# The gated convolution of a decoder trunk: c and v gates with the activations held stationary, their product turned through DRAM, the b gate last

## The chip, the core and the metric

The kernel runs on one core of a Trainium2 chip. A core has five engines, each with its own queue of instructions that it works through in order: PE multiplies matrices (the profile shows its loads of the stationary operand as a line of their own, PEld), DVE (VectorE) and ACT (ScalarE) work elementwise, POOL (GpSimd) too, and SP (SyncE) here issues transfers only. They meet through semaphores. On-chip memory is SBUF, with 128 partitions; PE writes its sums to PSUM, from where DVE and ACT fetch them. The metric is the time of one execution in microseconds (us), as the device measures it.

## What is computed

A trunk of two layers over 256 tokens of width 1024: one layer with a short gated convolution, one with sparse attention, each between two half-step SwiGLU feed-forward networks (FFNs). The change lies in the convolution and in one detail of the attention's bias tables.

```python
def short_conv_mixer(x, w_in, conv_w, w_out):
    b_gate, c_gate, v = jnp.split(x @ w_in, 3, axis=-1)
    u = c_gate * v
    y = lax.conv_general_dilated(u, conv_w[:, None, :], window_strides=(1,),
                                 padding=[(CONV_WIDTH - 1, 0)],
                                 dimension_numbers=('NWC', 'WIO', 'NWC'),
                                 feature_group_count=D_MODEL)
    return (b_gate * y) @ w_out
...
        hn = rmsnorm(h, mix_norm[i])
        if i < N_A_LAYERS:
            h = h + short_conv_mixer(hn, conv_w_in[i], conv_w[i], conv_w_out[i])
```

The convolution has three taps per channel and looks back in time: y[t] = w0 u[t-2] + w1 u[t-1] + w2 u[t].

## The kernel before

**Number format.** Every float32 operand of a product is split in a high part (rounded to the format PE takes, by a cast on ACT) and a low part (the rest, by a subtraction on DVE). A product of x and w is summed from high x high, low x high and high x low. The residual stream h lies channels on partitions, tokens along the row (8 tiles of 128 channels x 256 tokens); `xs[k]` holds tile k of the normed stream as [high 256 tokens | low 256 tokens]. The norm's factor, the inverse root mean square R of each token, is not multiplied in ahead of the products but behind them.

**Weights.** `Stream` (L116) brings all weights in the order of their use. A transfer on SP fetches a chunk of 128 x 2048 numbers into one of three `ws` buffers; each chunk is two units of 1024 columns. `high` (L146) casts a unit into a `wh` buffer on ACT, `low` (L171) makes its `wl` on DVE. At most six units (NBUF) are in being: `done` gives units back, and `pump` then makes as many new ones. Their instructions stand in ACT's and DVE's queues at the place where the code called `pump`.

**Two forms of a projection.** In the first (`a_pass`, L346) the weights are stationary: for each of eight k, a block of 128 x 128 high weights is loaded and the whole of `xs[k]` (512 columns) streams past (L351), and then for each k a block of low weights with the 256 high columns (L356). The result has channels on partitions, and its two halves must be added up. In the second form, used in the FFNs (`ffn_tokens`, L432 to L434) and in a part of their output projection (L493 to L495), the activations are stationary: for each k and each half of the tokens, three products with 512 weight columns. The result has tokens on partitions and is complete; it must be turned. `turned` (L386) and `placed` (L397) do that: DVE transposes blocks of 32 x 32, a transfer writes the tile to DRAM, and a second one reads it back in runs of 32 numbers, with channels on partitions.

**The convolution** (L713 to L751) uses the first form throughout. A loop over the eight tiles f of 128 channels takes three units each, in the order c, v, b: `a_group` (L375) gives PE 24 products of 512 and 24 of 256 columns; c and v go to a pair of PSUM banks, b to a single one. For f = 0, the norm's row R and its square R2 are made between two products (`conv_mid`, L739). Behind the products `conv_evac` (L713) is woven with the weights' preparation: after each `yield` one unit is made. It adds the halves of c and v (`total`, L362, ACT and DVE), multiplies them and R2 on POOL (L718, L719), adds b's halves (L721, L722) and multiplies with R on POOL (L723), applies the three taps (L727 on ACT, L728 and L729 on DVE), multiplies y and b (L731), and splits the result into z[f] (`split`, L358: cast L359 on ACT, subtraction L360 on DVE).

**What follows** is the output projection (`out_proj`, L471, without `rest`). Its first pass takes four units and runs the first seven of z for three tiles and the first two for the fourth (L351, L356), then the rest of each (L351, L356) and its evacuation (L455); the other four tiles run one by one (L533, L539). Between, the next FFN's weights are prepared.

**Tables.** `tables` (L259) is a generator in three steps that loads small constants and prepares the attention's bias rows. The convolution's loop takes the first two steps at f = 1 and f = 6; the second FFN takes the last one. `load_bias` (L760) then reads bias tiles from DRAM during that FFN, one transfer for each of two halves for tiles 0 to 5, one for both halves for 6 and 7.

`_layout` (L1390) puts the weights on the host in the order in which they are taken.

Of the kernel before, what the change touches and what calls it, by code (L numbers as in the profile page):

```python
# [9 lines left out]
F32 = mybir.dt.float32  # L10
F32R = mybir.dt.float32r
I32 = mybir.dt.int32
AF = mybir.ActivationFunctionType
# [55 lines left out]
def trunk(ctx, tc, A, out):  # L69
# [12 lines left out]
    def mk(shape, tag, bufs, dt=F32, pool=None):  # L82
        uid[0] += 1
        return (pool or sb).tile(list(shape), dt, tag=tag, name=f"{tag}_{uid[0]}", bufs=bufs)
# [12 lines left out]
    def bank(shape=(P, 512)):  # L97
        return mk(shape, "a", 4, pool=ps)

    def bank2():  # L100
        return mk([P, 2, 512], "mm", 2, pool=ps)

    def act(shape=(P, 512), dt=F32R):
        return mk(shape, "act", 22, dt)
# [4 lines left out]
    def t1(shape=(P, T)):  # L109
        return mk(shape, "t1", 6)  # L110
# [148 lines left out]
    def tables():  # L259

        sy.dma_start(small, A["small"])
        rb, oh = t2([P, P]), t2()
        po.memset(rb, 0.0)
        po.memset(rb[NB:NB + 1, :16], NEG)
        sy.dma_start(rb[:NB, :16], A["rel_bias"])
        po.memset(oh, 0.0)
        sy.dma_start(oh[:NB + 1], A["onehot"])
        yield
        ohr, rbr = act(), act([P, 2, P])
        po.tensor_copy(out=ohr, in_=oh)  # L270
        ac.copy(rbr[:, 0], rb)
        ve.tensor_tensor(out=rbr[:, 1], in0=rb, in1=rbr[:, 0].bitcast(F32), op=ALU.subtract)
        yield
        pr = bank()
        for x in range(2):
            pe.matmul(pr, rbr[:, x], ohr, start=(x == 0), stop=(x == 1))
        row = t2()
        ac.activation(row[:16], pr[:16], AF.Copy, scale=-1.0)
        sy.dma_start(row_d, row[:16])
# [78 lines left out]
    def split(src, dst):  # L358
        ac.copy(dst[:, :T], src)  # L359
        ve.tensor_tensor(out=dst[:, T:], in0=src, in1=dst[:, :T].bitcast(F32), op=ALU.subtract)  # L360

    def total(o, n):  # L362

        r = t2([P, n, T])
        ac.copy(r, o[:, :, T:])
        ve.tensor_tensor(out=r, in0=o[:, :, :T], in1=r, op=ALU.add)
        return r

    def weave(gen, rest=True):
        for _ in gen:  # L370
            W.pump(1)
        if rest:
            W.pump()
# [336 lines left out]
    out_proj(hid, 0.5, nm, rest=rest)  # L710
    nm.halves()

    def conv_evac(f, ocv, ob, R, R2, zs):  # L713
        r = total(ocv, 2)
        yield
        u = mk([P, 768], "pr", 6)[:, :T + 2]
        po.memset(u[:, :2], 0.0)
        po.tensor_tensor(out=u[:, 2:], in0=r[:, 0], in1=r[:, 1], op=ALU.mult)  # L718
        po.tensor_tensor(out=u[:, 2:], in0=u[:, 2:], in1=R2, op=ALU.mult)  # L719
        b = t1()  # L720
        ac.copy(b, ob[:, T:])  # L721
        ve.tensor_tensor(out=b, in0=ob[:, :T], in1=b, op=ALU.add)  # L722
        po.tensor_tensor(out=b, in0=b, in1=R, op=ALU.mult)  # L723
        yield
        tap = [gt[:, G_CONV + 8 * a + f:G_CONV + 8 * a + f + 1] for a in range(3)]
        y = t1()
        ac.activation(y, u[:, 2:], AF.Copy, scale=tap[2])  # L727
        ve.scalar_tensor_tensor(out=y, in0=u[:, 1:T + 1], scalar=tap[1], in1=y, op0=ALU.mult, op1=ALU.add)  # L728
        ve.scalar_tensor_tensor(out=y, in0=u[:, 0:T], scalar=tap[0], in1=y, op0=ALU.mult, op1=ALU.add)  # L729
        yield  # L730
        ve.tensor_tensor(out=y, in0=y, in1=b, op=ALU.mult)  # L731
        z = act()
        split(y, z)
        zs.append(z)

    zs = []
    box = [None]

    def conv_mid():  # L739
        R = nm.rows()  # L740
        R2 = mk([P, T], "R", 2)
        po.tensor_tensor(out=R2, in0=R, in1=R, op=ALU.mult)
        box[0] = R, R2

    tab = tables()
    for f in range(8):
        if f in (1, 6):
            next(tab)
        ob, ocv = bank(), bank2()
        a_group([ocv[:, 0], ocv[:, 1], ob], xs, conv_mid if f == 0 else None)  # L750
        weave(conv_evac(f, ocv, ob, *box[0], zs))  # L751

    xs = new_xs()
    nm = Norm([(xs, G_FFN2)])
# [5 lines left out]
    def load_bias(j):  # L760
        pp, hg = divmod(j, 4)
        b = kt8[:, j, T:].rearrange("p (a n) -> p a n", a=2)
        src = bass.AP(tensor=row_d.tensor, offset=row_d.offset + (8 * pp + hg) * OHW,
                      ap=[[1, P], [4 * OHW, 2], [1, 256]])
        for a in range(2):
            if a == 0 or j < 6:
                sy.dma_start(b[:, a:] if j > 5 else b[:, a], src[:, a:] if j > 5 else src[:, a])
        bias[j] = b

    def c_bias(j):  # L770
# [613 lines left out]
def _rows(w):  # L1384

    k, m = w.shape[0] // 128, w.shape[1] // 128
    return w.reshape(k, 128, m, 128).transpose(1, 2, 0, 3).reshape(128, -1)


def _layout(i):  # L1390
    a = {n: np.asarray(v) for n, v in i.items()}
    x = a["x"][0].T.reshape(8, 128, 256).transpose(1, 0, 2)
    r = {}
    for n in ("ffn1", "ffn2"):
        w = a[n + "_w_in"]
        ins, outs = [], []
        for w, v, turn in zip(w.reshape(2, 1024, -1), a[n + "_w_out"], (0, n == "ffn2")):
            ins.append(w.reshape(8, 128, 2, NF // 2, 256).transpose(1, 3, 0, 2, 4).reshape(128, -1))
            v = v.reshape(-1, 4, 2, 32, 1024).transpose(0, 2, 3, 1, 4).reshape(-1, 1024)
            if turn:  # L1400
                outs.append(v.reshape(NF, 128, 2, 512).transpose(1, 2, 0, 3).reshape(128, -1))
                continue
            first = v[:, :512].reshape(FF, 2, 2, 32, 4).transpose(0, 1, 4, 2, 3).reshape(NF, 128, 512).transpose(1, 0, 2)
            v = v[:, 512:].reshape(NF, 128, 4, 128).transpose(1, 2, 0, 3)
            outs.append(np.concatenate([x.reshape(128, -1) for x in (first, v)], 1))
        r[n + "_w_in"], r[n + "_w_out"] = np.stack(ins), np.stack(outs)

    w = r["ffn1_w_in"][0][:, :8192].reshape(128, 2, 8, 512)
    rows, second = np.concatenate([x, w[:, 0]], 2).reshape(128, -1), w[:, 1].reshape(128, -1)
    w = a["conv_w_in"][0].reshape(8, 128, 3, 8, 128)  # L1410
    r["conv_w_in"] = np.concatenate([w[:, :, 1:], w[:, :, :1]], 2).transpose(1, 3, 2, 0, 4).reshape(128, -1)
    r["conv_w_out"] = _rows(a["conv_w_out"][0])
    w = a["w_kv"].reshape(8, 128, 3, 2, 256)
    parts = [p.reshape(8, 128, 512).transpose(1, 0, 2).reshape(128, -1) for p in (w[:, :, 1:, 0], w[:, :, 1:, 1])]
    r["w_kv"] = np.concatenate(parts + [_rows(w[:, :, 0].reshape(1024, 512))], 1)
    for n in ("cmp_w1_k", "cmp_w1_v"):
        r[n] = a[n].reshape(2, 16, 64, 128).transpose(0, 2, 1, 3).reshape(128, -1)
    w = a["attn_w_q"][0]
    q = w[:, :1024].reshape(8, 128, 2, 512).transpose(2, 1, 0, 3).reshape(2, 128, -1)
    gates = w[:, 1024:].reshape(1024, 16, 3)  # L1420
    gates = np.concatenate([gates[:, :, 1:2], gates[:, :, 0:1], gates[:, :, 2:3]], 2).reshape(1024, 48)
    r["attn_w_q"] = np.concatenate(q, 1)
    r["attn_w_g"] = gates.reshape(8, 128, 48).transpose(1, 0, 2).reshape(128, -1)
    r["attn_w_o"] = a["attn_w_o"][0].reshape(2, 2, 4, 64, 8, 128).transpose(1, 3, 4, 0, 2, 5).reshape(128, -1)
    r["rel_bias"] = a["rel_bias"]
    cols = [a[n].reshape(-1, 128).T for n in ("ffn1_norm", "mix_norm", "ffn2_norm", "kv_norm", "conv_w")]
    cols += [np.concatenate([a[n].reshape(-1, 64)] * 2, 1).T for n in ("attn_q_norm", "k_norm")]
    cols += [np.zeros((128, G_N - sum(c.shape[1] for c in cols)), np.float32)]
    rows = np.concatenate(cols + [rows], 1)
    r["first"] = np.concatenate([(second[:, 512 * lo:512 * hi] if which else rows[:, lo:hi]).reshape(-1) for which, lo, hi, _ in PIECES])  # L1430
    cols = [np.eye(128, dtype=np.float32)]
    cols += [a[n].reshape(2, 16, 64).transpose(0, 2, 1).reshape(128, 16) for n in ("cmp_pe_k", "cmp_pe_v")]
    cols += [a["cmp_w2_k"], a["cmp_w2_v"]]
    cols += [np.repeat((np.arange(128) >= 31).astype(np.float32)[:, None], S_N - S_CM, 1)]
    r["small"] = np.concatenate(cols, 1)


    lim = [16, 23, 32, 46, 64, 91, 128, 182]
    oh = np.zeros((NB + 1, OHW), np.float32)
    for c in range(OHW):  # L1440
        d = c - 127
        oh[NB if d < 0 else d if d < 16 else 15 + sum(d >= x for x in lim), c] = 1.0
    r["onehot"] = oh
    return r
# [19 lines left out]
```

## Time and profile before

| what | us |
|---|---|
| median of 3 runs (950.53 to 950.8) | 950.73 |
| the profiled execution, its own time | 950.93 |
| its span, first to last instruction | 949.1 |
| PE busy in the span | 944.6 |
| DVE busy in the span | 657.5 |
| ACT busy in the span | 532.4 |
| POOL busy in the span | 138.8 |

The profile gives busy time by engine, by stretches of time and by groups of like instructions, and the chain of waits that ended last. In a group's row, the line is that of the program, then engine, operation, what it writes <- what it reads, shapes and count; behind the bar the busy time in us, the mean duration of one in ns, and the idle time of the engine ahead of them with what ended it. Matmuls are pipelined: the duration of one is its latency, and the pitch from start to start, which the chain shows (start, us, what, count), is what it costs a busy PE.

### The profile page before, as it was taken

The numbers are of one execution on the slowest core, as the hardware profiler recorded it, in microseconds if no ns is written. First come the engines' busy times: TensorE is split into PE (matmuls) and PEld (weight loads), VectorE is DVE, ScalarE is ACT, GpSimd is POOL, SyncE is SP. The second block draws the span as 40 slices with busy tenths as digits, with TensorE's granted clock in tenths as the row PEclk, the third lists the DMA queues.
The fourth block names the chain that finished last, engine by engine and source line by source line (L and its number), as shares of the span: only waits on it lengthen the run. The fifth ranks groups of instructions, "written<-read, shape, count | busy, mean of one in ns | idle before, by whom it ended". The sixth has DMA issues, their size and how long they took to land.

```text
span 949.1 us, 12899 instructions
## 1 busy us (share of the span) xinstructions
PE 944.6 (100%) x4674; PEld 792.3 (83%) x4674; DVE 657.5 (69%) x1058; ACT 532.4 (56%) x895; POOL 138.8 (15%) x215
## 2 busy tenths in 40 slices
PE   9999999999999999999999999999999999999998
PEld 7888888888888888888888888888877888888887
DVE  7766665778896677647756676865679786776662
ACT  7554544555565455545647774644589764544450
POOL 2000000244520010001221022200238120000000
PEclk9999999999999999999999999999999999999999
DMA  7778876645546998777646977876511247998770
GB/s 312 237 228 279 253 258 219 228 171 200 181 165 233 267 292 253 225 269 222 222 159 207 276 229 248 271 251 191 212 50 32 103 177 233 275 284 260 232 268 23
DMA packets 154380, 206.35 MB, mean 217 GB/s; under 512 B 115740, under 2 KB 131228, under 8 KB 133837
## 3 DMA queue, kind: packets, MB, share of 16 engines
q1 hardware_dynamic: 154172, 205.27, 66.3%
q8 instruction: 37, 0.61, 0.2%
q10 hardware_dynamic: 144, 0.26, 0.1%
q14 instruction: 27, 0.21, 0.1%
HBM read 189.75 MB, written 15.24 MB: 216 GB/s over the span
## 4 chain that ended last, share of the span: by engine, by line
PE 99%; DMA 1%; ACT 0%; SPq 0%; issue 0%; DVE 0%
PE mm L432 16%; PE mm L434 16%; PE mm L433 16%; PE a L533 7%; PE mm L351 4%; PE a L351 4%; PE a L539 4%; PE mm L493 3%; PE mm L494 3%; PE mm L495 3%; PE a L592 2%; PE a L590 2%; PE a L591 2%; PE mm L656 2%; PE a L356 2%; PE mm L356 2%
## 5 line engine op out<-in xcount | busy, mean ns | idle before, releaser
L183 DVE TENSOR_TENSOR wl<-ws,wh 128x1024 fp32r<-128x1024 f32 x316 | 390.5, 1255 | 209.4 <-ACT wh L166 192.2
L166 ACT CAST wh<-ws 128x1024 fp32r<-128x1024 f32 x316 | 324.6, 1048 | 219.7 <-DMA ws<-in_ffn_w_in_dram 99.0
L432 PE MATMUL mm<-wh,xs 128*128 128x512 f32 x656 | 256.2, 391 | 0.0
L434 PE MATMUL mm<-wl,xs 128*128 128x512 f32 x656 | 255.7, 390 | 0.0
L433 PE MATMUL mm<-wh,xs 128*128 128x512 f32 x656 | 255.6, 390 | 0.0
L434 PEld LDWEIGHTS mm<-wl,xs 128*128 128x128 f32 x656 | 123.2, 188 | 26.2 <-DVE wl L183 0.4
L433 PEld LDWEIGHTS mm<-wh,xs 128*128 128x128 f32 x656 | 123.3, 188 | 25.2
L432 PEld LDWEIGHTS mm<-wh,xs 128*128 128x128 f32 x656 | 123.3, 188 | 25.1
L311 POOL TENSOR_TENSOR sq<-sq,t 128x256 f32<-128x256 f32 x42 | 34.8, 829 | 384.6 <-ACT t L309 383.9
L390 ACT ACTIVATE t<-mm,rc 128x256 f32<-128x256 f32 x86 | 40.6, 472 | 56.2 <-DVE t L391 47.6
L533 PE MATMUL a<-act,wh 128*128 128x512 f32 x296 | 69.5, 390 | 0.0
L533 PEld LDWEIGHTS a<-act,wh 128*128 128x128 f32 x296 | 55.0, 188 | 10.9
L391 DVE SCALAR_TENSOR_TENSOR t<-mm,rc,t 128x256 f32<-128x256 f32 x86 | 41.4, 482 | 15.5 <-ACT t L390 12.0
L493 PE MATMUL mm<-wh,act 128*128 128x512 f32 x132 | 51.4, 390 | 0.0
L494 PE MATMUL mm<-wh,act 128*128 128x512 f32 x132 | 51.4, 389 | 0.0
L495 PE MATMUL mm<-wl,act 128*128 128x512 f32 x132 | 51.4, 389 | 0.0
L359 ACT CAST act<-t 128x256 fp32r<-128x256 f32 x96 | 34.6, 405 | 26.3 <-DVE t L731 19.4
L294 ACT ACTIVATE xs<-base 128x256 fp32r<-128x256 f32 x48 | 24.1, 505 | 43.0 <-DVE base L455 27.3
L392 DVE STREAM_TRANSPOSE t<-t 128x256 f32<-128x256 f32 x88 | 39.2, 445 | 3.1
L360 DVE TENSOR_TENSOR act<-t,act 128x256 fp32r<-128x256 f32 x96 | 37.1, 424 | 4.4 <-ACT act L359 4.4
L539 PEld LDWEIGHTS a<-act,wl 128*128 128x128 f32 x296 | 37.2, 192 | 1.0
L539 PE MATMUL a<-act,wl 128*128 128x256 f32 x296 | 37.5, 283 | 0.0
(279 smaller groups left out, 1203.6 us busy)
## 6 DMA issues: line engine op xcount, KB each, us to landing
ws<-in_ffn_w_in_dram SPq DMA_DIRECT2D x84, 1024.0 KB, 5.7
ws<-in_ffn_w_out_dram SPq DMA_DIRECT2D x44, 1024.0 KB, 6.2
ws<-in_conv_w_in_dram SPq DMA_DIRECT2D x12, 1024.0 KB, 4.6
turn<-t SPq DMA_DIRECT2D x44, 256.0 KB, 2.2
t<-turn SPq DMA_DIRECT2D x44, 256.0 KB, 7.2
ws<-in_w_kv_dram SPq DMA_DIRECT2D x6, 1024.0 KB, 5.8
ws<-in_conv_w_out_dram SPq DMA_DIRECT2D x4, 1024.0 KB, 5.0
ws<-in_attn_w_q_dram SPq DMA_DIRECT2D x4, 1024.0 KB, 4.9
```

What stands on the lines that cost most here:

```text
L166: ac.copy(h, src)
L183: ve.tensor_tensor(out=l, in0=src, in1=h.bitcast(F32), op=ALU.subtract)
L351: pe.matmul(o, u[0][:, k * P:(k + 1) * P], xs[k], start=(k == 0), stop=False)
L391: ve.scalar_tensor_tensor(out=s, in0=o[tt][:, T:], scalar=rc[:, tt:tt + 1], in1=s, op0=ALU.mult, op1=ALU.mult)
L432: pe.matmul(o[tt], sh, wh, start=(k == 0), stop=False)
L433: pe.matmul(o[tt], sl, wh, start=False, stop=False)
L434: pe.matmul(o[tt], sh, wl, start=False, stop=(k == 7))
L493: pe.matmul(o[:, tt], sh, wh, start=(k == 0), stop=False)
L494: pe.matmul(o[:, tt], sl, wh, start=False, stop=False)
L495: pe.matmul(o[:, tt], sh, wl, start=False, stop=(k == NF - 1))
L533: pe.matmul(o, run[k][0], lhs[k], start=(k == 0), stop=(k == last))
L539: pe.matmul(o[:, :T], run[k][1], lhs[k][:, :T], start=False, stop=(k == last))
```

## The change

- c and v take the second form: four groups n = 0 to 3 of 512 channels (c, v of the first half of the channels, then c, v of the second half), 48 products of 512 columns each (`conv_tokens`). c is copied from PSUM by ACT (`gate`); v is multiplied by it and by the square of R as a column (`r2`, made by way of a small write to and read from DRAM) on DVE, transposed there, and written to DRAM, 256 KB for each half of the tokens (`conv_turned`).
- The reading back (`conv_placed`, two transfers) is issued in group n = 2 at k = 3 for the first half, and at f = 1 of the b gate for the second.
- The taps (`conv_taps`) of tiles 0 to 2 run in group n = 3, of 3 behind it, of 4 and 5 at f = 5 and of 6 and 7 at f = 6. The padding's columns fall away: the two DVE products shorten to 254 and 255 columns. y, not b, is multiplied by R on POOL.
- The b gate follows alone, eight times one unit by `a_pass`. `conv_sum` adds its halves, `conv_product` multiplies with y, `conv_split` splits one tile later than before (f - 1 at f). Weights are pumped after the evacuation, for f = 0 to 4 and 7 only.
- The evacuations of the c and v groups stand ahead of the weights' preparation in the queues.
- `load_bias`: tiles 4 and 5 are also read by one transfer.
- The host lays `conv_w_in` out anew.

```diff
-    def conv_evac(f, ocv, ob, R, R2, zs):
...
+    zs, Y, conv = [], [], {}
+    tab = tables()
+
+    def conv_tokens(o, step):
+
+        for k in range(8):
+            if k % 2 == 0:
+                u, = W.take()
+            wh, wl = [u[x][:, (k % 2) * 512:(k % 2 + 1) * 512] for x in range(2)]
+            for tt in range(2):
+                sh, sl = xs[k][:, tt * P:(tt + 1) * P], xs[k][:, T + tt * P:T + (tt + 1) * P]
+                pe.matmul(o[:, tt], sh, wh, start=(k == 0), stop=False)
+                pe.matmul(o[:, tt], sl, wh, start=False, stop=False)
+                pe.matmul(o[:, tt], sh, wl, start=False, stop=(k == 7))
+            if k % 2 == 1:
+                W.done(1, k < 7)
+            step(k)
+
+    def conv_turned(gate, o):
+        d = mk([2, 2, P, T], "conv", 2, pool=dr)
+        for tt in range(2):
+            tb = t2()
+            ve.scalar_tensor_tensor(out=gate[tt], in0=o[:, tt], scalar=conv["r2"][:, tt:tt + 1], in1=gate[tt],
+                                    op0=ALU.mult, op1=ALU.mult)
+            ve.transpose(tb, gate[tt])
+            sy.dma_start(d[:, tt].rearrange("m p n -> p m n"), tb.rearrange("p (m n) -> p m n", m=2))
+        return d
+
+    def conv_placed(d):
+        r = []
+        for m in range(2):
+            r.append(t2([P, 2, T]))
+            sy.dma_start(r[m].rearrange("p c (b j) -> p c b j", j=32),
+                         d[m].rearrange("t (b i) (x c j) -> (i x) c (t b) j", i=32, c=2, j=32))
+        return r
+
+    def conv_taps(f):
+
+        m, c = divmod(f, 2)
+        if c == 0:
+            Y.append(act([P, 2, T], F32))
         tap = [gt[:, G_CONV + 8 * a + f:G_CONV + 8 * a + f + 1] for a in range(3)]
...
+        u, y = conv["u", m // 2][m % 2][:, c], Y[m][:, c]
+        ac.activation(y, u, AF.Copy, scale=tap[2])
+        for a in range(2):
+            ve.scalar_tensor_tensor(out=y[:, 2 - a:], in0=u[:, :T - 2 + a], scalar=tap[a], in1=y[:, 2 - a:],
+                                    op0=ALU.mult, op1=ALU.add)
+        po.tensor_tensor(out=y, in0=y, in1=conv["R"], op=ALU.mult)
...
+    def conv_step(n, k):
+        if n == 0 and k == 5:
+            conv["R"] = R = nm.rows()
+            rd, rc, conv["r2"] = mk([1, T], "rd", 1, pool=dr), mk([P, 2], "rc", 2, pool=tiny), sm([P, 2])
+            sy.dma_start(rd, R[:1])
+            sy.dma_start(rc, rd.rearrange("o (t p) -> (o p) t", t=2))
+            po.tensor_tensor(out=conv["r2"], in0=rc, in1=rc, op=ALU.mult)
+        if n == 1 and k == 1:
+            next(tab)
+        if n == 2 and k == 3:
+            conv["u", 0] = conv_placed(conv.pop(("d", 0)))
+        if n == 2 and k == 5:
+            next(tab)
+        if n == 3 and k in (2, 4, 6):
+            conv_taps(k // 2 - 1)
+
+    for n in range(4):
+        o = bank2()
+        conv_tokens(o, lambda k: conv_step(n, k))
+        if n % 2 == 0:
+            gate = [t2() for _ in range(2)]
+            for tt in range(2):
+                ac.copy(gate[tt], o[:, tt])
+        else:
+            conv["d", n // 2] = conv_turned(gate, o)
+            del gate
+        W.pump()
+    conv_taps(3)
+    bs = {}
+
+    def conv_sum(f, o):
+        bs[f] = b = t1()
+        ac.copy(b, o[:, T:])
+        ve.tensor_tensor(out=b, in0=o[:, :T], in1=b, op=ALU.add)
+
+    def conv_product(f):
+        ve.tensor_tensor(out=bs[f], in0=bs[f], in1=Y[f // 2][:, f % 2], op=ALU.mult)
+
+    def conv_split(f):
+        zs.append(act())
+        split(bs.pop(f), zs[f])
+
     for f in range(8):
...
+        o, (u,) = bank(), W.take()
+        a_pass([(o, u, xs, range(8))])
+        W.done(1, False)
+        if f == 1:
+            conv["u", 1] = conv_placed(conv.pop(("d", 1)))
+        if f < 5:
+            if f:
+                conv_split(f - 1)
+            conv_sum(f, o)
+            if f < 4:
+                conv_product(f)
+            W.pump()
+        elif f == 5:
+            conv_taps(4)
+            conv_taps(5)
+            conv_sum(5, o)
+            conv_product(4)
+        elif f == 6:
+            conv_split(4)
+            conv_taps(6)
+            conv_taps(7)
+            conv_product(5)
+            conv_sum(6, o)
+        else:
+            conv_split(5)
+            conv_product(6)
+            conv_split(6)
+            conv_sum(7, o)
+            conv_product(7)
+            conv_split(7)
+            W.pump()
...
-            if a == 0 or j < 6:
-                sy.dma_start(b[:, a:] if j > 5 else b[:, a], src[:, a:] if j > 5 else src[:, a])
+            if a == 0 or j < 4:
+                sy.dma_start(b[:, a:] if j > 3 else b[:, a], src[:, a:] if j > 3 else src[:, a])
```

More of the change, by code (lines that the diff above doesn't have):

```diff
@@ L711, in trunk @@
     nm.halves()
-    def conv_evac(f, ocv, ob, R, R2, zs):
[L714 to L724, printed above, removed]
-        tap = [gt[:, G_CONV + 8 * a + f:G_CONV + 8 * a + f + 1] for a in range(3)]
[L726 to L745, printed above, removed]
-    for f in range(8):
[L747 to L751, printed above, removed]
+    zs, Y, conv = [], [], {}
+    tab = tables()
@@ new lines, in conv_taps @@
+    def conv_taps(f):
+        m, c = divmod(f, 2)
+        if c == 0:
+            Y.append(act([P, 2, T], F32))
+        tap = [gt[:, G_CONV + 8 * a + f:G_CONV + 8 * a + f + 1] for a in range(3)]
+        u, y = conv["u", m // 2][m % 2][:, c], Y[m][:, c]
[4 more added lines that the diff above has]
+        po.tensor_tensor(out=y, in0=y, in1=conv["R"], op=ALU.mult)
+        if f % 4 == 3:
+            del conv["u", m // 2]
@@ L753, in trunk @@
+    conv.clear()
+    del o, u
     xs = new_xs()
@@ L1409, in _layout @@
     rows, second = np.concatenate([x, w[:, 0]], 2).reshape(128, -1), w[:, 1].reshape(128, -1)
-    w = a["conv_w_in"][0].reshape(8, 128, 3, 8, 128)
-    r["conv_w_in"] = np.concatenate([w[:, :, 1:], w[:, :, :1]], 2).transpose(1, 3, 2, 0, 4).reshape(128, -1)
+    w = a["conv_w_in"][0]
+    cv = w[:, 1024:].reshape(8, 128, 2, 2, 2, 2, 32, 4).transpose(1, 3, 2, 0, 4, 7, 5, 6).reshape(128, -1)
+    r["conv_w_in"] = np.concatenate([cv, _rows(w[:, :1024])], 1)
     r["conv_w_out"] = _rows(a["conv_w_out"][0])
```

## The prediction

> **What bounds the kernel now.** I read the page first, then the chain of waits in order of time, then sums over windows.
>
> ```profile
> span 949.1 us, 12899 instructions
> ...
> PE 944.6 (100%) x4674; PEld 792.3 (83%) x4674; DVE 657.5 (69%) x1058; ACT 532.4 (56%) x895; POOL 138.8 (15%) x215
> ...
> 186.17:253.13 66.96, 66.96 (x388) 59.29 (x387) 55.53 (x71) 36.26 (x57) 32.56 (x37) 1.00 0.57 201
> 236.62:244.96 8.34, 8.34 (x49) 7.39 (x49) 7.53 (x11) 4.61 (x9) 4.72 (x5) 1.00 0.49 145
> 49.55:103.95 54.40, 54.40 (x242) 45.08 (x240) 36.70 (x53) 27.35 (x42) 0.00 (x0) 1.00 0.77 246
> ```
>
> The columns of a window row are its length, then busy time and instructions of PE, PEld, DVE, ACT and POOL, the granted clock, and the DMA. PE (the matmuls) is busy the whole 66.96 us of the convolution (186.17 to 253.13) at clock 1.00; in one of its eight groups DVE is busy 7.53 of 8.34 us, but nobody on PE waits for it. So only two things can move the time: matmuls that PE no longer pays for, and matmuls that begin to wait. The chain gives the price of a matmul by its shape, as pitch from start to start (a single matmul's "mean ns" is its latency):
>
> ```profile
> 244.96 3.65 PE mm L351 x16
> ...
> 250.43 1.91 PE mm L356 x16
> ...
> 264.45 1.84 PE a L533 x8
> 266.29 0.95 PE a L539 x8
> ```
>
> 512 columns cost about 0.227 us (L351, 3.65/16), 256 columns 0.12 us (L356, 1.91/16). The rows from 264.45 are one tile of the output projection: eight products of each kind, in the same order as a gate's tile.
>
> **The change, part by part.**
>
> *Matmuls.* Before, a tile of one gate costs eight products of 512 and eight of 256 columns; the eight groups of three parts fill 66.96 us, 0.24 us of which are the two products of the norm (2 x 0.12). After, c and v take four groups of 48 products of 512 columns. That form already runs in the first FFN: the window 49.55 to 103.95 is five groups of 48, 54.40/240 = 0.2267 us each, so a group costs 10.88 us and four 43.52. The b gate alone is eight groups like the one at 264.45: 1.84 + 0.95 = 2.79 us each, 22.32 in all. Sum 43.52 + 22.32 + 0.24 = 66.08 us: **0.88 us less**. The columns streamed are equal (192 x 512 after, 128 x 768 before); what goes is the dearer pitch of the short products (0.12 is more than half of 0.227).
>
> ```profile
> L434 PEld LDWEIGHTS mm<-wl,xs 128*128 128x128 f32 x656 | 123.2, 188 | 26.2 <-DVE wl L183 0.4
> ```
>
> The weight loads fall from 256 to 192 for c and v. One takes 188 ns (row above), yet load and product together repeat every 0.2267 us, so the load lies beside the product and I cost it at nothing. [...]
>
> *Vector and scalar work under the products.* The rows by group (busy time, then mean ns of one) and of two DMA issues (KB, then us to landing):
>
> ```profile
> L183 DVE TENSOR_TENSOR wl<-ws,wh 128x1024 fp32r<-128x1024 f32 x316 | 390.5, 1255 | 209.4 <-ACT wh L166 192.2 <-PE a L539 8.1 <-PE mm L434 6.6
> L166 ACT CAST wh<-ws 128x1024 fp32r<-128x1024 f32 x316 | 324.6, 1048 | 219.7 <-DMA ws<-in_ffn_w_in_dram 99.0 <-DMA ws<-in_ffn_w_out_dram 49.3 <-PE mm L494 25.2
> ...
> L360 DVE TENSOR_TENSOR act<-t,act 128x256 fp32r<-128x256 f32 x96 | 37.1, 424 | 4.4 <-ACT act L359 4.4
> ...
> L359 ACT CAST act<-t 128x256 fp32r<-128x256 f32 x96 | 34.6, 405 | 26.3 <-DVE t L731 19.4 <-DMA t<-turn 6.9
> ...
> L727 ACT ACTIVATE t<-pr,base 128x256 f32<-128x256 f32 x8 | 4.1, 510 | 9.5 <-POOL pr L719 9.5
> ...
> L501 DVE STREAM_TRANSPOSE pr<-mm 128x512 f32<-128x512 f32 x6 | 3.9, 692 | 0.0
> ...
> L331 DVE RECIPROCAL R<-t 128x256 f32<-128x256 f32 x2 | 3.5, 1753 | 3.7 <-ACT t L329 3.7
> ...
> L731 DVE TENSOR_TENSOR t<-t,t 128x256 f32<-128x256 f32 x8 | 3.3, 419 | 0.0
> ...
> L722 DVE TENSOR_TENSOR t<-a,t 128x256 f32<-128x256 f32 x8 | 3.3, 411 | 0.0
> ...
> L721 ACT COPY t<-a 128x256 f32<-128x256 f32 x8 | 3.0, 371 | 0.0
> ...
> L878 POOL TENSOR_TENSOR act<-t,R 128x256 f32<-128x256 f32 x4 | 3.0, 738 | 24.3 <-DVE t L877 24.3
> ...
> L329 ACT ACT_TABLE_LOAD x2 | 2.6, 1283 | 0.0
> ```
>
> ```profile
> ws<-in_conv_w_in_dram SPq DMA_DIRECT2D x8, 1024.0 KB, 4.6
> ...
> t<-in_rel_bias_dram SPq DMA_DIRECT2D x1, 2.0 KB, 1.6
> ```
>
> In c and v, DVE has 16 weight units of 1.25 us (L183), the gate product and transpose of four 512-wide tiles (about 0.69 each, so 5.5) and four taps of 1.0: 29.5 us in 43.5. Five prepared units stand ahead, 5 x 2.73 us of matmuls, so this is covered. The norm's turn to columns is (Sqrt after a table load) 1.3 + 0.5, 1.75 for the reciprocal, behind one cast of 1.05; then a write and a read of DRAM, which no row shows in this size. The nearest row is rel_bias, 1.6 us to landing, so 4.6 + 3.2 = 7.8 us from the end of k = 5 in the first group; with the medians of the large transposed transfers (2.2 and 7.2, rows below) it is 14. Two steps and one group, 2.7 + 10.9 = 13.6 us, remain until the first gate product wants it, and if that came late DVE would only eat into the five units ahead. I take nothing (the row nearest in size). Leaving out two bias DMAs in the second FFN is nothing: no engine waits for them. These DMAs go through SP in order, and only weights stand behind them, two chunks ahead.
>
>
> *The end of the stage.* Here a wait arises. The output projection reads z0 to z6 at once: with E the end of f = 7's pitch, z4 is wanted at E+0.9, z5 at E+1.14, z6 at E+1.36. Before, DVE's last group left z6 ready in time: its split ran at 252.28 and the projection began at 253.13.
>
> ```profile
> 252.28 0.43 DVE L360 TENSOR_TENSOR act<-t,act 128x256 fp32r<-128x256 f32 x1 [0.47 <-ACT act L359]
> ...
> 253.13 5.40 PE L351 MATMUL a<-act,wh 128*128 128x512 f32 x23
> ```
>
> After, four taps (f = 4 to 7) stand on DVE in the last 8.4 us, each two products of 0.48 (L729 when alone), and each is followed by POOL's product with R (0.74 alone, L878). How the two disturb each other shows here:
>
> ```profile
> 212.94 0.74 POOL L718 TENSOR_TENSOR pr<-t 128x256 f32<-128x256 f32 x1 [3.97 <-DVE t L366]
> 213.12 1.65 DVE L183 TENSOR_TENSOR wl<-ws,wh 128x1024 fp32r<-128x1024 f32 x1 [0.26 <-ACT wh L166]
> 213.76 1.50 POOL L719 TENSOR_TENSOR pr<-pr,R 128x256 f32<-128x256 f32 x1
> ...
> 215.02 1.32 DVE L183 TENSOR_TENSOR wl<-ws,wh 128x1024 fp32r<-128x1024 f32 x1
> 215.22 1.72 POOL L723 TENSOR_TENSOR t<-t,R 128x256 f32<-128x256 f32 x1
> 216.27 0.96 DVE L728 SCALAR_TENSOR_TENSOR t<-pr,base,t 128x256 f32<-128x256 f32 x1
> ...
> 217.26 0.48 DVE L729 SCALAR_TENSOR_TENSOR t<-pr,base,t 128x256 f32<-128x256 f32 x1
> ```
>
> Whichever starts first keeps going and the other stands still, all but its first 0.2 us or so: L723 begins at 215.22, ends at 216.94 once L183 is gone (216.34), and L728 behind it takes 0.96 instead of 0.48. An engine's next instruction, where it needs nothing from the one before, starts some 0.08 us before that one's end; a handover takes 0.03 to 0.05.
>
> With these rules and the durations above I lay out DVE in its program order, in us from E (f = 4's sums can be read at -8.2, the last product lasting 0.16 beyond its pitch): sum 4 to -7.3; the weight unit behind ACT's cast (-7.9 to -6.8), -6.8 to -5.55; taps 4 to -4.6; taps 5 to -3.6; sum 5 to -3.2; product 4, held up by POOL, to -2.6; split 4 (ACT 0.4, then DVE) to -1.7; taps 6 to -0.7; taps 7, held up by POOL, to +0.4; product 5 to 0.7; sum 6 to 1.05; split 5 by ACT 0.8 to 1.2 and by DVE to 1.65; product 6 to 2.0; split 6 by ACT to 2.45 and by DVE to 2.9. So z5 comes 0.57 us after it is wanted (with 0.06 to hand over), and z6 another 1.05 late: **1.6 us of waiting**. Nothing later is late too: z7 is ready at 4.7 and the next weights at 6.4, both wanted after E+7. Bounds of this term: 1.1 us with no port conflict at all, 2.8 if every DVE instruction with two SBUF inputs takes twice its time whenever POOL works (L728's ratio). I take 1.6, which the row at 215.22 to 217.22 reproduces.
>
> *Sum.* 950.93 (the profiled execution's time, its span 949.1 and 1.8 around it) - 0.88 + 1.6 = 951.65; from the median of the runs, 950.73, it is **951.5 us**. A measurement can tell about 0.2% (1.9 us) from no change, so this is "same".
>
> **Rivals.** *No wait* (z5 and z6 in time, because DVE runs ahead of my list): 950.73 - 0.88 = 949.9. For it: POOL does four products at the end, not the 1.6 us ones of before all along. Against it: two splits with two handovers each follow one another after tap 7.
>
> *The turned product lands late: slower.* The second half's rereading must land before ACT reaches tap 4, at 15.4 us after the end of the fourth c/v group (that is E-22.35).
>
> ```profile
> L394 SPq DMA_DIRECT2D turn<-t x44: 366/377/1549, 29.7 to 892.5; - x44
> ...
> DMA to landing us min/median/max: 2.1/2.2/5.9
> ...
> L399 SPq DMA_DIRECT2D t<-turn x44: 591/594/3762, 34.9 to 894.6; - x44
> ...
> DMA to landing us min/median/max: 3.4/7.2/10.2
> ```
>
> The FFN's same path (256 KB written, 256 KB reread in runs of 32 numbers) has medians 2.2 and 7.2: after 2.9 us of gate products and transposes it lands at 2.9 + 2.2 + 7.2 = 12.3, 3 us early. With the longest of both rows it is 2.9 + 5.9 + 10.2 = 19.0. From about 16 on, each us late is a us of PE, so 19.0 adds some 2.9 to the 1.6: 950.73 - 0.88 + 4.5 = 954.4; it is slower than 0.2% from a landing at 17.2. For it: two rereads stand in one row on SP, behind a weight chunk. Against it: PE never waited for 44 such turns. [...]
>
> *The loads count: faster.* If a weight load lay in the open, c and v would save 64 x 0.188 = 12 us more by the row: 950.73 - 0.88 - 12 = 938. The pitch of 0.2267 speaks against it. [...]
>
> *The change doesn't save what it says*: c and v pitch as L351 does, 0.228, costing 0.2 more: inside the forecast.
>
> **How the numbers follow.** Forecast (wait of 0.9 to 2.7) 0.58; no wait 0.16; late landing or a later DVE than listed, over the bound, 0.23; loads count 0.03. Same = 0.58 + 0.16 = 0.74, slower 0.23, faster 0.03. The range goes from no wait, 949.8, to 953.4, which takes in the dearest port (951.5 + 1.2 = 952.7) and landings up to about 18; some 0.1 lies above, 0.04 below.
>
> **What would show it.** Four c/v groups of 10.88 us, b groups of 2.79; PE idle before the sixth and seventh product of the output projection's first tile, released by DVE's split; taps 6 and 7 on DVE past the end of f = 7. Wrong would be: PE waiting inside c or v, ACT's tap 4 released by a DMA, or no idle time at the projection.

## The result, and the profile after

The changed kernel takes 956.7 us (median of 6 runs, 955.05 to 957.54) against 950.73 (6 runs, 950.49 to 951.17): ratio 1.006, 95% interval 1.0047 to 1.0073. It is **6 us slower**, outside the predicted range (949.8 to 953.4). The profiled execution took 957.54 us, its span is 955.8, so 6.7 more than before.

The page of the changed kernel, first span and busy time, then the slices with PE's busy tenths and the granted clock:

```profile
span 955.8 us, 12778 instructions
...
PE 947.3 (99%) x4610; PEld 790.8 (83%) x4610; DVE 652.5 (68%) x1058; ACT 532.7 (56%) x891; POOL 110.8 (12%) x191
...
PE   9999999999899999999999999999999999999998
...
PEclk9999999999899999999999999999999999999999
```

One slice of forty has both a gap on PE and a lower clock. It holds the start of the output projection. Windows over the convolution, and over the projection's head up to its fifth tile (length; busy time of PE, PEld, DVE, ACT, POOL; clock; DMA):

```profile
186.24:252.36 66.12, 66.12 (x324) 55.95 (x323) 48.38 (x63) 33.03 (x47) 8.70 (x14) 1.00 0.71 236
252.36:257.11 4.75, 1.60 (x7) 0.76 (x5) 4.07 (x10) 1.88 (x5) 1.70 (x3) 1.00 0.00 0
257.11:263.94 6.83, 6.32 (x14) 4.70 (x15) 5.26 (x9) 3.92 (x6) 0.00 (x0) 0.50 0.15 37
263.94:270.90 6.96, 6.96 (x47) 6.34 (x47) 2.40 (x7) 1.70 (x4) 0.00 (x0) 1.00 0.64 267
```

The convolution now takes 66.12 us instead of 66.96 and PE never waits in it: the gain is there, 0.84 us. The head, 252.36 to 270.90, takes 18.54 us; before, from 253.13 to the fifth tile's first product at 264.29, it took 11.16. The timeline row of before:

```profile
264.29 1.09 PE L533 MATMUL a<-act,wh 128*128 128x512 f32 x4
```

These 7.4 us, less the 0.84 gained, are the loss: 6.5 of the span's 6.7. They are of two kinds. In the first 4.75 us PE works 1.60. In the next 6.83 us it works almost all the time, but at clock 0.50: its products come every 0.427 us instead of 0.227 (the timeline's row at 258.42 has 13 in 5.79 us, the last one's latency included).

The timeline of the stage's end, PE and DVE, with ACT's rows from f = 4 on:

```profile
244.30 0.37 ACT L796 COPY t<-a 128x256 f32<-128x256 f32 x1
...
247.11 1.05 ACT L166 CAST wh<-ws 128x1024 fp32r<-128x1024 f32 x1 [2.45 <-DMA ws<-in_conv_w_out_dram]
248.06 0.91 ACT L756 ACTIVATE act<-t,base 128x256 f32<-128x256 f32 x2
248.19 1.23 DVE L183 TENSOR_TENSOR wl<-ws,wh 128x1024 fp32r<-128x1024 f32 x1 [2.43 <-ACT wh L166]
...
249.34 2.27 DVE L758 SCALAR_TENSOR_TENSOR act<-t,base,act 128x254 f32<-128x254 f32 x4
...
251.86 0.90 DVE L800 TENSOR_TENSOR t<-t,act 128x256 f32<-128x256 f32 x1
252.36 1.09 PE L351 MATMUL a<-act,wh 128*128 128x512 f32 x4
...
253.64 2.26 DVE L758 SCALAR_TENSOR_TENSOR act<-t,base,act 128x254 f32<-128x254 f32 x4
253.71 0.50 PE L351 MATMUL a<-act,wh 128*128 128x512 f32 x1 [0.25 <-DVE act L360]
...
257.19 0.80 PE L351 MATMUL a<-act,wh 128*128 128x512 f32 x1 [2.97 <-DVE act L360]
...
258.42 5.79 PE L351 MATMUL a<-act,wh 128*128 128x512 f32 x13 [0.44 <-DVE act L360]
```

PE waits where the prediction put it, for the splits of z5 and z6 (DVE L360), and for that of z4 as well, which the prediction had in time. They come 1.3, 4.8 and 6.0 us after the end of f = 7 (E, here 252.36; PE's starts behind them show it, 257.19 - 252.36 = 4.83), where the list had -1.7, 1.65 and 2.9. From pitch to pitch the three waits cost 0.42, 3.25 and 1.0 us, 4.7 in all. The row at 247.11 says where most of that starts: at f = 4 ACT stands 2.45 us on a weight chunk that has not landed, and all of taps 4 to 7 (L756, then L758 on DVE) stand behind that cast. SP's queue tells why it landed late:

```profile
234.21 0.41 SPq L139 DMA_DIRECT2D ws<-in_conv_w_out_dram  x1
235.98 4.20 SPq L745 DMA_DIRECT2D t<-conv  x2
240.28 5.16 SPq L139 DMA_DIRECT2D ws<-in_conv_w_out_dram  x3
```

The two rereads (L745) hold SP for 4.2 us, and the chunk is issued only behind them, at 240.28; with the 6.7 us that a chunk of this kind takes to land here (the page's median) it is in place at 247.0.

### The profile page after: what moved, and what is told of

It reads as the page before. It is cut to its first block, busy times and chain, and to the rows that moved or that the text cites. A ratio compares the mean times of both kernels' runs of the same rounds, so it can differ in the third digit from the quotient of the medians.

```text
span 955.8 us, 12778 instructions
## 1 busy us (share of the span) xinstructions
PE 947.3 (99%) x4610; PEld 790.8 (83%) x4610; DVE 652.5 (68%) x1058; ACT 532.7 (56%) x891; POOL 110.8 (12%) x191
## 4 chain that ended last, share of the span: by engine, by line
PE 95%; DVE 2%; DMA 1%; issue 1%; ACT 1%; SPq 0%; DVEq 0%; ACTq 0%
PE mm L432 16%; PE mm L434 16%; PE mm L433 16%; PE a L533 7%; PE a L539 4%; PE mm L494 3%; PE mm L493 3%; PE mm L495 3%; PE a L351 2%; PE a L592 2%; PE a L590 2%; PE a L591 2%; PE mm L656 2%; PE mm L725 1%; PE mm L724 1%; PE mm L726 1%
## 5 line engine op out<-in xcount | busy, mean ns | idle before, releaser
L360 DVE TENSOR_TENSOR act<-t,act 128x256 fp32r<-128x256 f32 x96 | 37.0, 423 | 1.6 <-ACT act L359 1.4
```

## The experiments

**Theory A**: the chunk behind the rereads on SP delays ACT and with it the last taps; with DVE's order at the end that makes PE wait 4.7 us, and the idle PE then loses half its clock (0.50 over 6.83 us). **Rival B**: the last taps on DVE, beside POOL, take that long by themselves. **Rival C**, the prediction's own: the rereading lands late.

**First: the chunk ahead of the rereads.**

```diff
-        if f == 1:
-            conv["u", 1] = conv_placed(conv.pop(("d", 1)))
         if f < 5:
...
             W.pump()
+            if f == 1:
+                conv["u", 1] = conv_placed(conv.pop(("d", 1)))
```

> The weights' preparation of f = 1 is put ahead of the second half's rereading, so that SP issues the next weight chunk before the two rereads instead of behind them; nothing else changes. Theory A (in the changed kernel ACT stands 2.45 us at f = 4 on a chunk whose transfer SP could issue only after the rereads' 4.2 us; all of taps 4 to 7 stand behind that cast; PE then waits 4.7 us and its clock falls to half for 6.8 us): no wait of ACT on the chunk, z5 and z6 some 2.4 us earlier against the end of f = 7 (about 2.4 and 3.6 us after it instead of 4.8 and 6.0), PE waits about 2.3 us in all, the clock stays at 1.00, time 950.7 - 0.84 + 2.3 = 952.2 (951.4 to 952.8). Rival B (the last taps on DVE against POOL are that long by themselves): z5 and z6 unchanged, time 955 to 957. Rival C (the rereading lands late): tap 4 on ACT now waits for a reread, time 954 to 957.

Measured: 953.23 us (9 runs, 951.89 to 954.01; before beside it 950.61; ratio 1.0024, interval 1.0014 to 1.0034). z5 and z6 come 2.25 and 3.49 us after E, and the cast ahead of the taps no longer waits for a DMA (a timeline row, without a wait):

```profile
243.82 1.05 ACT L166 CAST wh<-ws 128x1024 fp32r<-128x1024 f32 x1
```

E is 251.64 here, so this cast runs from -7.8 to -6.8 us, which is where the prediction's list has it. Rivals B and C fall as the cause of these 2.5 us. PE's waits sum to 2.2 us, as expected, but the time was missed by 1 us: the clock fell here too, for half as long. PE's timeline of this run, then its windows:

```profile
253.94 0.51 PE L351 MATMUL a<-act,wh 128*128 128x512 f32 x1 [0.98 <-DVE act L360]
...
255.18 5.74 PE L351 MATMUL a<-act,wh 128*128 128x512 f32 x17 [0.72 <-DVE act L360]
```

```profile
252.75:256.16 3.41, 1.70 (x6) 1.05 (x6) 2.52 (x7) 1.22 (x4) 0.78 (x1) 1.00 0.00 0
...
256.16:259.58 3.42, 3.42 (x9) 2.64 (x8) 2.60 (x3) 3.11 (x4) 0.00 (x0) 0.50 0.00 0
```

PE was idle half of the 3.41 us up to 256.16, and the next 3.42 us ran at half the clock. The runs fall in groups: four at 951.9 to 952.3, which is 950.61 - 0.84 + 2.2 = 952.0 with no fall of the clock, and five at 953.2 to 954.0, one fall dearer. Their mean granted clocks agree: 1.00 in the four, 0.998 in the five.

**Second: PE kept busy in the wait.** Twelve products into a spare bank between the head's fifth and sixth product.

```diff
+            spare = bank2()[:, 0]
+            for _ in range(12):
+                pe.matmul(spare, head[0][1][0][:, :P], lhs[0], start=True, stop=True)
```

> Twelve products into a spare PSUM bank (2.7 us at full clock, results unused) stand between the projection's fifth and sixth product, where PE waits 3.25 us in the changed kernel; everything else as there. If the clock's fall comes from PE's idleness: the clock stays at 1.00, z4 to z6 come at the same times (1.3, 4.8, 6.0 us after the end of f = 7), the 13 products at 0.427 us go back to 0.227, time 956.7 - 2.7 = 954.0 (953.5 to 954.6). If the fall has another cause, or if the waits alone make the loss: the products at 0.427 us stay, time 956 to 957 or above.

Measured: 954.18 us (5 runs, 953.03 to 954.45; ratio 1.0034, 1.0021 to 1.0047). z4 to z6 come at 1.4, 4.9 and 6.1 us, as late as in the changed kernel, and the clock stays whole over the head (a window row):

```profile
251.82:267.88 16.06, 14.74 (x78) 11.93 (x77) 11.83 (x23) 7.51 (x15) 1.81 (x3) 1.00 0.34 123
```

The head takes 16.06 us instead of 18.54 with twelve products more. The mean granted clock is 1.00 in all five runs; in the changed kernel's six it is 0.996 (four) or 0.998 (two). So the half clock follows from the idle PE, and is worth 2.5 us.

**Third: another order of products in the projection's head.**

```diff
-            a_pass([(o, u, lhs, range(n)) for (o, u), n in zip(head, cut)])
+            a_pass([(o, u, lhs, range(4)) for o, u in head[:3]])
+            for k in range(4, 7):
+                a_pass([(o, u, lhs, [k]) for o, u in head[:3]])
+            a_pass([(head[3][0], head[3][1], lhs, range(cut[3]))])
```

> The projection's first pass takes tiles 0 to 2 with z0 to z3, both kinds of products (4.2 us), then z4, z5, z6 for the three tiles each, then the fourth tile's part; the evacuations and the weights are as in the changed kernel. Theory A: z4, z5 and z6 (1.3, 4.8, 6.0 us after the end of f = 7) are wanted at 4.2, 5.2 and 6.3 only, so these waits go; the fourth tile's unit, cast at about 8.3 and ready at 9.5, is wanted at 7.3, so 1 to 2 us of waiting move there; the clock stays at 1.00; time 950.7 - 0.84 + 1.8 = 951.7 (950.8 to 952.4). If the loss were in the c and v groups or in anything but the projection's start, it would stay at 955 to 957.

Measured: 952.93 us (8 runs, 951.12 to 954.37; ratio 1.0022, 1.0012 to 1.0033), half a microsecond above the expected range. No product waits for a split any more, but another wait came that I had not seen, where a wait of 1 to 2 us for the fourth tile's unit was expected. A row of this run's list of waits (who waited, for whom: us in total, times, longest):

```profile
PE a L351 <- DVE t L800: 2.5, 1, 2.5
```

L800 in this kernel is the addition that empties b's PSUM bank of f = 6. The third tile reuses that bank, and wants it 1.8 us after E already; the sum stands on DVE behind the late taps 6 and 7, like everything else.

**Fourth: the weight unit of f = 4 behind product 4.** SP's order is that of the changed kernel, the chunk lands late as there.

```diff
             if f < 4:
                 conv_product(f)
-            W.pump()
+                W.pump()
...
             conv_product(4)
+            W.pump(1)
```

> The weight unit that f = 4 prepares ahead of taps 4 and 5 is prepared behind product 4 of f = 5; SP's order stays as in the changed kernel, so the chunk still lands late. Theory A: ACT's tap 4 no longer stands behind the cast that waits for the chunk and starts at the end of f = 4 (some 7.5 us before the end of f = 7 instead of 4.3), z5 and z6 come about 1 and 2.3 us after that end, PE waits 1 us or less, clock 1.00, time 950.7 - 0.84 + 0.9 = 950.8 (950.0 to 951.8). Rival B (the taps themselves): at most the unit's 1.2 us on DVE is won, time 954 to 956. Rival C (the rereading): tap 4 now waits for the reread, time 953 to 956.

Measured: 951.52 us (10 runs, 951.37 to 953.23; ratio 1.0011, 1.0002 to 1.0021). ACT's tap 4 starts at 244.31, with no wait for a weight or for a reread (rival C falls once more); z5 and z6 come at 1.6 and 2.84 us, some 0.6 later than expected; PE waits 0.5 us for the first and 1.0 for the second, the clock stays whole (1.00 in all ten runs), the head takes 12.80, 1.64 more than before (a timeline row and a window row):

```profile
244.31 0.91 ACT L756 ACTIVATE act<-t,base 128x256 f32<-128x256 f32 x2
...
252.13:264.93 12.80, 11.73 (x67) 9.76 (x66) 9.13 (x18) 6.04 (x11) 0.90 (x2) 1.00 0.43 157
```

950.61 - 0.84 + 1.64 = 951.4, 0.1 below the measured time. So letting the taps pass the cast that waits brings z5 and z6 forward by 3.2 us with SP's order untouched: 2.5 as in the first experiment, and more because DVE's part of that unit (1.2 us) now stands behind the taps too.

**Fifth: what POOL costs at the end.** The first experiment's kernel without the products of y and R for tiles 4 to 7.

```diff
-        po.tensor_tensor(out=y, in0=y, in1=conv["R"], op=ALU.mult)
+        if f < 4:
+            po.tensor_tensor(out=y, in0=y, in1=conv["R"], op=ALU.mult)
```

> The first experiment's kernel (weights ahead of the rereads) without POOL's product of y and R for tiles 4 to 7, which leaves the norm's factor out of half the channels. It measures what POOL beside DVE costs at the end: there product 4 took 0.91 us instead of 0.42, four taps products 2.27 instead of 4 x 0.48. Expected if the two block one another: z5 about 0.6 to 0.9 us earlier than there (1.4 to 1.6 us after the end of f = 7 instead of 2.25), z6 at 2.5 to 2.8 instead of 3.49; PE waits some 1.4 instead of 2.2 us, clock mostly 1.00, time 951.2 (950.6 to 952). If POOL costs DVE nothing, z5 and z6 and the time are as in the first experiment (951.9 to 954.0).

Measured: 950.85 us (10 runs, 950.46 to 952.66; before beside it 950.95). Each of the two groups of four taps products takes 1.92 us instead of 2.27, product 4 takes 0.42 instead of 0.91, z5 and z6 come at 1.07 and 2.30 instead of 2.25 and 3.49, PE waits 1.1 us. POOL beside DVE therefore costs 1.2 us of the splits' delay, more than the 0.6 to 0.9 expected.

**Sixth: the bias tiles alone**, on the kernel before.

> The kernel before with the bias tiles' change alone (tiles 4 and 5 by one transfer each). Every theory: no difference, 950.4 to 950.9; a difference of more than 0.3 us would mean that a part of the loss lies in the second FFN.

Measured: 950.94 us (10 runs) beside 950.95: no difference.

**Seventh: DVE's order mended.** The first and the fourth edit, and the order of the last tiles:

```diff
         elif f == 6:
             conv_split(4)
-            conv_taps(6)
-            conv_taps(7)
             conv_product(5)
+            conv_taps(6)
+            conv_split(5)
             conv_sum(6, o)
         else:
-            conv_split(5)
             conv_product(6)
             conv_split(6)
+            conv_taps(7)
             conv_sum(7, o)
```

> The changed kernel with SP's order of the first experiment, the weight unit of the fourth one behind product 4, and the last tiles' order changed to split 4, product 5, taps 6, split 5, sum 6 at f = 6 and product 6, split 6, taps 7, sum 7, product 7, split 7 at f = 7. Theory A (the loss is DVE's and ACT's order at the end, nothing else): z5 is ready at or before the end of f = 7 and z6 about 1.6 us after it, so PE waits 0.3 us, the clock stays at 1.00, time 950.6 - 0.84 + 0.3 = 950.1 (949.7 to 950.7), faster than or equal to the kernel before. If c and v in the new form cost PE anything that the stage's length hides, or the clock falls without a wait, 951 or above.

Measured: 950.77 us (11 runs, 950.37 to 952.73) beside 950.95; ratio 1.0001, 0.9993 to 1.001. z5 comes 0.2 us before E and z6 1.74 after it; the head takes 12.02 us, 0.9 above before instead of 0.3, because z6 was waited for 0.44 us and the fourth tile, whose high weights ACT casts late, another 0.3.

**Eighth: both orders**, the seventh with the third experiment's head.

> The previous run's kernel with the projection's head of the third experiment (z0 to z3 for three tiles first). Theory A: no wait of PE is left; the head takes its 11.15 us as before the change, the convolution 66.13, and the time is 950.6 - 0.84 = 949.8 (949.5 to 950.2), the whole of the form's gain. If the third tile's bank or unit comes late (it is wanted 1.8 us after the end of f = 7), up to 1 us more.

Measured: 949.88 us (11 runs, 949.53 to 950.46) beside 950.95 (33 runs); ratio 0.9992, interval 0.9983 to 1.0001. PE waits nowhere; the windows over convolution and head:

```profile
185.60:251.73 66.13, 66.13 (x324) 55.94 (x323) 51.21 (x69) 34.56 (x51) 9.19 (x15) 1.00 0.72 237
251.73:262.92 11.19, 11.19 (x66) 9.82 (x65) 8.54 (x16) 5.67 (x9) 1.14 (x2) 1.00 0.30 106
```

Convolution and head together are 77.32 us, against 66.96 + 11.16 = 78.12 before. This version is 1.1 us below the kernel before by the medians and 0.8 by the profile; the interval just reaches 1, so that it is faster at all rests mainly on the profile's windows.

## Why the prediction was wrong, point by point

- **The matmuls' gain was right**: 0.88 predicted, 0.84 measured. The rival of 938 us, weight loads in the open, did not appear.
- **The place of the wait was right**, its size not: 1.6 us predicted, 4.7 measured. Of the 3.1 us between, the first experiment takes away 2.5 (its waits sum to 2.2); the other 0.6 are POOL's.
- **The failed step** is the list's entry "the weight unit behind ACT's cast (-7.9 to -6.8)". It takes that cast's chunk as landed; the only reason given is the sentence on the new transfers in SP's queue, "only weights stand behind them, two chunks ahead", and nothing is taken for what the rereads hold up there. That sentence holds for PE, which did not run out of weights. What ran late was ACT, which casts a unit as soon as its buffer is free, long before PE wants it, and has the taps behind that cast. The cast ran at -5.25 to -4.2. The first experiment, which only changes SP's order, brings it back to -7.8 and z5 and z6 forward by 2.5 us each; the fourth, which moves the unit behind the taps, brings them forward by 3.2.
- **A term was missing**: the clock. The sum had every product at the full clock because all rows of before show 1.00, but in the stretches that they cover PE is never idle, so that they cannot show what a wait does. It cost 2.5 us (second experiment). The fall lasted 6.83 us in the changed kernel and 3.42 in the first experiment, where PE was not idle all the time ahead of it: it was busy 1.70 of the last 3.41 us.
- **The cost of POOL beside DVE was mis-sized**: with the weights in time, z5 and z6 came at 2.25 and 3.49 us (first experiment), 0.6 later than the list. The fifth experiment shows that POOL makes the splits 1.2 us later, where the list had 0.5. Without POOL's products PE waits 1.1 us (12.24 us of head, 11.16 before), the prediction's own bound for no conflict.
- **The rival that came out slower**, a late rereading, comes nearer in price (954.4 us forecast, 956.7 measured) but has not the mechanism: the rereads landed 5.5 to 8.0 us after their issue and no engine waited for them. It was what SP issued behind them that came late.
- By windows: -0.84 for the convolution, +4.7 for waits, +2.7 for products at half clock, together +6.6 of the span's +6.7.

## What to carry to other kernels

A new transfer on an in-order queue must be checked against the first engine that uses what stands behind it, not against the engine that bounds the kernel: prefetch that is far ahead of PE can be just in time for the engine that prepares it (here SP issued the chunk behind 4.2 us of rereads, and ACT, not PE, stood 2.45 us on it). Where a kernel keeps PE busy without a gap, a wait costs its length and perhaps a stretch at half clock behind it (6.83 us long in the changed kernel's profile, 3.42 in the first experiment's), so a forecast that puts a wait on PE should name that price. Here waits of 4.7 us in all brought the half clock in every run, waits of 2.2 and 2.5 us (first and third experiment) in some, and the 1.5 us of the fourth in none. A projection's order of products is a cheap place to hide late operands, as long as the PSUM banks it wants earlier are free: with the other head PE waited nowhere in the eighth experiment, and 2.5 us for a bank in the third.

## What the runs showed of the hardware that was not expected

In the first experiment's profile the clock fell behind 1.7 us of idle time, in two pieces of 0.98 and 0.72 us within 3.41 us, while in the third one wait of 2.5 us brought no fall (clock 1.00 over its head; but three of that kernel's eight runs have a mean clock of 0.998).

Nor does the work ahead of a fall tell the two apart. Counted by their pitch, PE's products filled 0.2 us of the 3.41 us ahead of the fall in the changed kernel (253.70 to 257.11) and 1.2 us in the first experiment (252.75 to 256.16). In the third experiment they filled 0.8 us of the 3.41 us up to the end of its wait (253.05 to 256.46), and no fall followed. The first experiment's kernel itself ran with the fall in five executions and without it in four. What decides stays open: no run was made for it.
